# Attention of a two-layer decoder trunk: heads by quarters, with the projections cut into pieces between the heads' stages

## The chip, the cores and the metric

One core of a Trainium2 chip runs the whole program in one launch. The metric is the device time of one execution in microseconds. Before the change it was 1347.86 us, the median of 3 runs (1347.23 to 1348.67).

## The reference, cut to what matters

The input is a sequence of 512 tokens of width 1024 in float32. Layer 0 is a recurrent mixer (an RG-LRU and a Mamba-2 SSD side by side) followed by a dense SwiGLU network; layer 1 is an attention layer followed by a second SwiGLU network. The change is in the attention layer alone:

```python
h = rmsnorm(x, norm_g)
qkv = (h @ w_qkv).reshape(b, l, 3, 16, 64)
q = partial_rope(rmsnorm(qkv[:, :, 0], q_norm), pos) * (64 ** -0.5)   # rope on the first 16 of 64
k = partial_rope(rmsnorm(qkv[:, :, 1], k_norm), pos)
v = qkv[:, :, 2]
# softmax attention over three dilated windows, (128, 1), (512, 4), (2048, 16),
# merged by their softmax denominators
...
return x + o @ w_out
```

There are 16 heads of 64 channels. The three windows are merged into one softmax: the kernel adds the logarithm of how many windows hold a key (a table `lnc`, -1e30 where none does) to the scores.

## The kernel before, in words

Every large product is made in three parts to keep float32 precision: each operand is split into a rounded high part and a low part, and the matmuls xh\*wl, xl\*wh and xh\*wh are added up in PSUM. A weight tile of 128x1024 is loaded by a DMA on SP's queue (line 105), its high part is cast by ScalarE and its low part is subtracted by VectorE, or by GpSimd for the attention weights (lines 87 to 91). `weight(i)` returns tile i and at the same time issues tile i+2; three tiles of each kind are held.

In the attention layer the queries, keys and values are projected for 8 heads at a time (`qkv_part`, a half): the stationary operand is a 128-token block of the input, the moving operand 512 columns of the weight. `finish_qk` then works on one 128-token block of q or k: ScalarE scales the block and squares it, VectorE sums the squares per head, GpSimd raises them to -1/2, VectorE multiplies and makes six small rotary operations. `pair_T` transposes q and k of two heads (four transposes each) and splits them into high and low parts; both parts of q lie on the 128 rows that the array sums over, so that two matmuls make a block of scores instead of three. `scores(h)` makes the four blocks of query rows of one head (128, 256, 384 and 512 keys wide, causal), and then for each a custom VectorE reduction, a ScalarE exponential, a reciprocal, and a GpSimd multiplication by it. `values(h)` transposes the probabilities in three groups (`P_AT`), splits each, and multiplies them with v. `out_proj` makes two output tiles of 128 channels from one weight tile and four pairs of heads.

The order written is: the three projections of half 0, its 8 heads, the three projections of half 1, its 8 heads with the first half's output projection between them, and the second half's output projection. This order is not the one in which the engines run: the framework keeps a list of what is written, and puts an instruction on its engine when its inputs are ready by the framework's own estimate, earlier written ones first. Each engine then runs its list in order, and waits on semaphores. So the projections of half 1 run between the heads of half 0.

PSUM has eight banks: four for projections (`pa`), three for transposes and scores (`pm`), one for the values' sums (`po`). Lines that the steps below touch: 96 to 109 (`weight`), 709 (rotary tables), 721 to 743 (projections), 747 to 768 (`finish_qk`), 770 to 788, 790 to 796 (`finish_v`), 806 to 860, 862 to 898.

Of the kernel before, what the change touches and what calls it, by code (L numbers as in the profile page):

```python
# [58 lines left out]
def trunk(ctx: ExitStack, tc: tile.TileContext, a):  # L59
# [36 lines left out]
    def weight(i):  # L96
        while emitted[0] <= min(i + AHEAD, len(specs) - 1):
# [11 lines left out]
        return w_of.pop(i, None)  # L109
# [578 lines left out]
    with ExitStack() as actx:  # L688
# [9 lines left out]
        tabs = {}  # L698
        for w, (gn, rn, scale) in enumerate((("q_gain", "q_rope", 0.125), ("k_gain", "k_rope", 1.0))):
# [5 lines left out]
            g1 = pc(rn, 0, 8).rearrange("p (o e) -> p o e", o=1).to_broadcast([P, NT, 8])  # L705
            g2 = pc(rn, 8, 8).rearrange("p (o e) -> p o e", o=1).to_broadcast([P, NT, 8])
            for nm, trig, gg in (("c1", cos, g1), ("s2", sin, g2), ("c2", cos, g2), ("s1", sin, g1)):
                t = am.tile([P, NT, 8], F32, name=f"rope{w}{nm}", bufs=1)
                V.tensor_tensor(out=t, in0=trig, in1=gg, op=ALU.mult)
                tabs[w, nm] = t  # L710

        qkT = {}
        vt = {}


        kz = [[ap_.tile([P, T], F32R, name=f"kz{b}{e}") for e in range(2)] for b in range(2)]
# [4 lines left out]
        def qkv_part(half, w):  # L721

            pss = []

            def step(kp):
                if kp == 0:
                    for t in range(NT):
                        pss.append(pa.tile([P, T], F32, tag="pa", name="ps_qkv"))
                wh, wl = weight(i_qkv[half, w, kp])
                for t in range(NT):  # L730
                    ts_ = slice(t * P, (t + 1) * P)
                    for k2 in range(2):
                        k = 2 * kp + k2
                        xh, xl = norm.hl[k]
                        cols = slice(k2 * T, (k2 + 1) * T)
                        mm(pss[t], lhsT=xl[:, ts_], rhs=wh[:, cols], start=(k == 0), stop=False)  # L736
                        mm(pss[t], lhsT=xh[:, ts_], rhs=wl[:, cols], start=False, stop=False)  # L737
                        mm(pss[t], lhsT=xh[:, ts_], rhs=wh[:, cols], start=False, stop=(k == KD - 1))  # L738
                if kp == 3:
                    for t in range(NT):  # L740
                        (finish_v if w == 2 else finish_qk)(half, w, t, pss[t])

            return [lambda kp=kp: step(kp) for kp in range(4)]

        qk = {}

        def finish_qk(half, w, t, ps):
            q = at.tile([P, 8, 64], F32, tag=f"q{w}{t}", name="q", bufs=2)
            qf = q.rearrange("p h e -> p (h e)")
            S.activation(qf, ps, AF.Copy, scale=norm.rt[:, t:t + 1])  # L750
            sq = at.tile([P, 8, 64], F32, tag="qsq", name="qsq", bufs=1)
            S.activation(sq.rearrange("p h e -> p (h e)"), qf, AF.Square)
            ss = am.tile([P, 8], F32, tag="qss", name="qss")
            V.tensor_reduce(out=ss, in_=sq, axis=AX.X, op=ALU.add)
# [10 lines left out]
            V.tensor_tensor(out=tmp[:, 3], in0=x1, in1=tb("s1"), op=ALU.mult)  # L765
            V.tensor_tensor(out=x1, in0=tmp[:, 0], in1=tmp[:, 1], op=ALU.subtract)  # L766
            V.tensor_tensor(out=x2, in0=tmp[:, 2], in1=tmp[:, 3], op=ALU.add)
            qk[half, w, t] = q

        def pair_T(pair):  # L770
            half, p = pair // 4, pair % 4
# [221 lines left out]
```

## Time and profile before

| | |
|---|---|
| runs, median | 1347.86 us |
| profiled execution, own time | 1346.39 us |
| its span, first to last instruction | 1344.6 us |
| PE (matmul) busy | 1318.4 us, 98% |
| PEld (weight load) busy | 1072.5 us, 80% |
| DVE (VectorE) busy | 796.2 us, 59% |
| ACT (ScalarE) busy | 573.4 us, 43% |
| POOL (GpSimd) busy | 151.7 us, 11% |
| granted TensorE clock | 0.999 of full speed |

The profiled execution is 1.47 us below the median of the runs, and its span is 1.8 us shorter than its own time. Matmuls are pipelined: one is shown as 0.39 us long where the next starts 0.23 us later, so the busy share of PE says that it seldom stood still, and not that it ran at its best spacing. The spacing of the starts is what to read. The attention layer is the stretch from 717 to 978 us.

### The profile page before, as it was taken

Reading aid. Unit: us, or ns where it says so; the run is one execution under the profiler, and the core shown is the slowest. Engines: PE = TensorE matmul, PEld = TensorE weight load, DVE = VectorE, ACT = ScalarE, POOL = GpSimd, SP = SyncE. Lnnn points to the kernel's source line nnn. Section 1 sums busy time; section 2 is a strip of 40 time slices with the busy share of each in tenths; the row PEclk is TensorE's granted clock in tenths of the full one; section 3 lists DMA queues with packets and bytes.
Section 4 is the critical chain, followed back from the end, with each engine's and each line's share of the span. In section 5 each row is a group of like instructions: output and inputs, shape, how many; then the busy total and the mean of one; then the engine's idle time right before and its main releaser. Section 6 shows DMA issues by size and latency. Waiting matters only on the chain.

```text
span 1344.6 us, 15688 instructions
## 1 busy us (share of the span) xinstructions
PE 1318.4 (98%) x6058; PEld 1072.5 (80%) x6058; DVE 796.2 (59%) x1332; ACT 573.4 (43%) x842; POOL 151.7 (11%) x130
## 2 busy tenths in 40 slices
PE   8999989999999999999999999999999999999998
PEld 6877767788888888888888877777788888888887
DVE  6886799975454434434453778788764434443442
ACT  5743867443333222322243379558643212222321
POOL 0000000000000000000005755554300000000000
PEclk9999999999999999999999999999999999999999
DMA  6322222532323323233232221121032323323232
GB/s 239 111 80 93 95 79 71 174 101 94 94 94 94 95 96 102 89 106 94 89 100 94 90 68 47 63 78 48 32 108 96 94 95 96 100 87 110 94 95 78
DMA packets 38555, 126.50 MB, mean 94 GB/s; under 512 B 4289, under 2 KB 5057, under 8 KB 38353
## 3 DMA queue, kind: packets, MB, share of 16 engines
q1 hardware_dynamic: 38480, 125.51, 29.2%
q8 instruction: 47, 0.77, 0.2%
q14 instruction: 28, 0.22, 0.0%
HBM read 123.36 MB, written 2.13 MB: 93 GB/s over the span
## 4 chain that ended last, share of the span: by engine, by line
PE 81%; DVE 9%; ACT 6%; POOL 2%; issue 1%; DMA 0%; SPq 0%; POOLq 0%; DVEq 0%; ACTq 0%
PE ps_pr L113 24%; PE ps_pr L114 24%; PE ps_pr L115 24%; ACT s L825 2%; POOL qrs L757 1%; DVE q L758 1%; PE ps_qkv L738 1%; PE ps_qkv L737 1%; PE ps_qkv L736 1%; DVE q L766 1%; ACT ph L90 1%; PE ps_o L852 1%; PE ps_pT L845 1%; ACT qk_hi L783 1%; DVE rtmp L762 1%
## 5 line engine op out<-in xcount | busy, mean ns | idle before, releaser
L90 ACT CAST wh<-wr 128x1024 fp32r<-128x1024 f32 (+2 forms) x223 | 228.2, 1025 | 621.3 <-PE ps_pr L115 388.2
L113 PE MATMUL ps_pr<-xh,wl 128*128 128x512 f32 x1056 | 416.5, 395 | 12.7 <-DVE wl L91 12.0
L114 PE MATMUL ps_pr<-xl,wh 128*128 128x512 f32 x1056 | 414.5, 392 | 0.9 <-DVE xl L191 0.9
L115 PE MATMUL ps_pr<-xh,wh 128*128 128x512 f32 x1056 | 413.2, 391 | 0.0
L91 DVE TENSOR_TENSOR wl<-wr,wh 128x1024 fp32r<-128x1024 f32 (+2 forms) x191 | 225.6, 1182 | 52.3 <-ACT wh L90 51.9
L113 PEld LDWEIGHTS ps_pr<-xh,wl 128*128 128x128 f32 x1056 | 199.4, 189 | 55.5 <-DVE wl L91 12.9
L114 PEld LDWEIGHTS ps_pr<-xl,wh 128*128 128x128 f32 x1056 | 199.5, 189 | 43.5 <-DVE xl L191 1.8
L115 PEld LDWEIGHTS ps_pr<-xh,wh 128*128 128x128 f32 x1056 | 199.3, 189 | 42.4 <-issue 0.6
L113 PE MATMUL ps_pr<-ah,wl 128*128 128x512 f32 x352 | 136.9, 389 | 0.0
L114 PE MATMUL ps_pr<-al,wh 128*128 128x512 f32 x352 | 136.9, 389 | 0.0
L115 PE MATMUL ps_pr<-ah,wh 128*128 128x512 f32 x352 | 136.9, 389 | 0.0
L91 POOL TENSOR_TENSOR wl<-wr,wh 128x1024 fp32r<-128x1024 f32 x32 | 78.4, 2453 | 392.3 <-ACT wh L90 392.2
L670 DVE TENSOR_TENSOR tu<-ps_pr,nrb 128x512 f32<-128x512 f32 x44 | 30.4, 691 | 130.7 <-PE ps_pr L115 130.7
L678 DVE TENSOR_TENSOR x<-ps_pr,x 128x512 f32<-128x512 f32 x48 | 33.2, 692 | 120.4 <-PE ps_pr L115 120.3
L668 DVE TENSOR_TENSOR tg<-ps_pr,nrb 128x512 f32<-128x512 f32 x44 | 30.4, 691 | 94.1 <-PE ps_pr L115 94.1
L114 PEld LDWEIGHTS ps_pr<-al,wh 128*128 128x128 f32 x352 | 66.1, 188 | 13.8
L115 PEld LDWEIGHTS ps_pr<-ah,wh 128*128 128x128 f32 x352 | 66.1, 188 | 13.7
L113 PEld LDWEIGHTS ps_pr<-ah,wl 128*128 128x128 f32 x352 | 66.1, 188 | 13.7
L736 PE MATMUL ps_qkv<-wh,xl 128*128 128x512 f32 x192 | 75.6, 394 | 0.5 <-ACT q L750 0.5
L737 PE MATMUL ps_qkv<-wl,xh 128*128 128x512 f32 x192 | 75.5, 393 | 0.0
L738 PE MATMUL ps_qkv<-wh,xh 128*128 128x512 f32 x192 | 75.5, 393 | 0.0
L736 PEld LDWEIGHTS ps_qkv<-wh,xl 128*128 128x128 f32 x192 | 36.1, 188 | 7.9 <-ACT q L750 1.0
(233 smaller groups left out, 1575.2 us busy)
## 6 DMA issues: line engine op xcount, KB each, us to landing
wr<-in_w_gu SPq DMA_DIRECT2D x88, 512.0 KB, 3.5
wr<-in_w_in SPq DMA_DIRECT2D x35, 512.0 KB, 3.5
wr<-in_w_dn SPq DMA_DIRECT2D x32, 448.0 KB, 3.2
wr<-in_w_qkv SPq DMA_DIRECT2D x24, 512.0 KB, 3.5
wr<-in_w_out SPq DMA_DIRECT2D x16, 512.0 KB, 3.5
wr<-in_w_dn SPq DMA_DIRECT2D x16, 512.0 KB, 3.4
x<-in_xT SPq DMA_DIRECT2D x16, 256.0 KB, 3.7
bcs<-csd SPq DMA_DIRECT2D x16, 256.0 KB, 4.4
```

Of the source, the lines that this page charges most:

```text
L90: S.copy(hi, src)
L91: eng.tensor_tensor(out=lo, in0=src, in1=hi.bitcast(F32), op=ALU.subtract)
L113: mm(ps, lhsT=wl[ws], rhs=xh[xs], start=start, stop=False)
L114: mm(ps, lhsT=wh[ws], rhs=xl[xs], start=False, stop=False)
L115: mm(ps, lhsT=wh[ws], rhs=xh[xs], start=False, stop=stop)
L668: V.tensor_tensor(out=tg, in0=pg, in1=rb, op=ALU.mult)
L670: V.tensor_tensor(out=tu, in0=pu, in1=rb, op=ALU.mult)
L678: V.tensor_tensor(out=x[m], in0=ps, in1=x[m], op=ALU.add)
L736: mm(pss[t], lhsT=xl[:, ts_], rhs=wh[:, cols], start=(k == 0), stop=False)
L737: mm(pss[t], lhsT=xh[:, ts_], rhs=wl[:, cols], start=False, stop=False)
L738: mm(pss[t], lhsT=xh[:, ts_], rhs=wh[:, cols], start=False, stop=(k == KD - 1))
L825: S.activation(s, s, AF.Exp, scale=-1.0, bias=m[:, 0:1], accum_out=m[:, 1:2])
```

## The change

The attention layer is rewritten; everything ahead of it and behind it stays.

- q, k and v are projected for 4 heads at a time (a quarter). One weight tile holds 256 columns of q and 256 of k for two blocks of the inner dimension, so q and k of a quarter are still matmuls of 512 columns. v of a quarter has 256 columns, and its matmuls are 256 wide: 384 of them, where there were 192 of 512.
- The projections are lists of short pieces: a piece of q and k is 6 matmuls of 512 columns (one token block, two inner blocks), one of v is 12 of 256 columns (one token block, four inner blocks), one of the output projection is 6 of 512. `fill_in` writes the next pieces between the steps of the heads.
- Heads go by pairs. A pair's twelve steps hold the transposes and values of both its heads and, between them, `pair_T` and `scores` of the next pair. With each pair 12 pieces are written for the first five, then 4, 5 and 4.
- q and k of a quarter are finished together: one power on GpSimd for 128x32 sums in place of four for 128x8, four multiplications, and four rotary operations over all four token blocks with two prepared tables (32 small multiplications at the start, where there were 8). Of these the VectorE operations are written through a queue, two behind each piece.
- `scores` takes both heads of a pair together, in three groups, with two PSUM banks at a time; one reciprocal serves a group. The transposed probabilities have one buffer of each kind instead of two.
- A weight tile two ahead is issued behind the second piece of the tile in work, instead of ahead of its first.

The diff, cut to its core (removed functions stand in the listing above):

```diff
     def weight(i):
-        while emitted[0] <= min(i + AHEAD, len(specs) - 1):
+        weight_emit(i + AHEAD)
+        return weight_get(i)
+    def weight_get(i):
+        return w_of.pop(i, None)
+    def weight_emit(i):
...
-    i_qkv = {}
-    for half in range(2):
-        for w in range(3):
-            for kp in range(4):
-                i_qkv[half, w, kp] = add_spec(a["w_qkv"][w * 2 + half, kp], D)
+    i_qkv = {(g, c): add_spec(a["w_qkv"][g, c], D) for g in range(4) for c in range(6)}
...
+        cc = at.tile([P, NT, 8, 16], F32, name="rope_c", bufs=1)
+        sc = at.tile([P, NT, 8, 16], F32, name="rope_s", bufs=1)
...
+            for half in range(2):
...
+                for t in range(NT):
+                    for tab, trig, gx in ((cc, cos, gg), (sc, sin, ng)):
+                        V.tensor_tensor(
+                            out=tab[:, t, 4 * w:4 * w + 4, es],
+                            in0=trig[:, t].rearrange("p (o e) -> p o e", o=1).to_broadcast([P, 4, 8]),
+                            in1=gx.rearrange("p (o e) -> p o e", o=1).to_broadcast([P, 4, 8]), op=ALU.mult,
+                        )
...
+        def qk_pieces(g):
...
+            def piece(kp, t):
+                i = i_qkv[g, kp]
+                if t == 0:
+                    w_cur[i] = weight_get(i)
...
+                    mm(pss[t], lhsT=xl[:, ts_], rhs=wh[:, cols], start=(k == 0), stop=False)
...
+                if t == 1:
+                    weight_emit(i + AHEAD)
+                if kp == 3:
+                    finish_a(t)
+            def finish_a(t):
...
+                S.activation(qf, pss[t], AF.Copy, scale=norm.rt[:, t:t + 1])
...
+                S.activation(sq.rearrange("p h e -> p (h e)"), qf, AF.Square)
+                queue.append(lambda: V.tensor_reduce(out=sqs["ss"][:, t], in_=sq, axis=AX.X, op=ALU.add))
+                if t == NT - 1:
+                    queue.append(finish_b)
...
+            def finish_b():
...
+                G.tensor_tensor(out=rs.rearrange("p t h -> p (t h)"), in0=ss, in1=mhalf[:, :NT * 8], op=ALU.pow)
+            def finish_c(t):
...
+                V.tensor_tensor(out=q, in0=q, in1=sqs["rs"][:, t].rearrange("p (h o) -> p h o", o=1).to_broadcast([P, 8, 64]), op=ALU.mult)
...
+            def finish_d():
...
+                V.tensor_tensor(out=c, in0=q[:, :, 0:16], in1=cc.rearrange("p t h e -> p (t h) e"), op=ALU.mult)
+                V.tensor_tensor(out=s, in0=q[:, :, 0:16], in1=sc.rearrange("p t h e -> p (t h) e"), op=ALU.mult)
+            def finish_e():
+                q, c, s = views()
+                V.tensor_tensor(out=q[:, :, 0:8], in0=c[:, :, 0:8], in1=s[:, :, 8:16], op=ALU.add)
+                V.tensor_tensor(out=q[:, :, 8:16], in0=c[:, :, 8:16], in1=s[:, :, 0:8], op=ALU.add)
...
         def v_pieces(g):
...
+            def piece(vp, t):
...
+                ps = pss[t][:, :256]
+                for k4 in range(4):
...
+                    mm(ps, lhsT=xl[:, ts_], rhs=wh[:, cols], start=(k == 0), stop=False)
...
+                if vp == 1:
+                    v = ap_.tile([P, 4, 2, 64], F32R, tag=f"v{t}", name="v", bufs=2)
...
+            return [lambda vp=vp, t=t: piece(vp, t) for vp in range(2) for t in range(NT)]
...
+        S_AT = {0: ((3, 0),), 1: ((0, 0), (2, P)), 2: ((1, 0),)}
+        P_AT = {0: ((0, 0),), 1: ((1, 0), (3, 3 * P)), 2: ((2, 0),)}
...
+        def scores(p, b):
...
+            pss = [pm.tile([P, T], F32, tag="pm", name="ps_s") for _ in range(2)]
+            for i, c in S_AT[b]:
...
+                    mm(pss[e][:, c:c + n], lhsT=q[e][:, qs], rhs=kl[e][:, :n], start=True, stop=False)
+                    mm(pss[e][:, c:c + n], lhsT=q[e][:, qs], rhs=kh[e][:, :n], start=False, stop=True)
...
+                    if c == 0:
+                        prob[2 * p + e, "s", b] = at.tile([P, WID[b]], F32, tag=f"s{b}", name="s", bufs=4)
...
+                    V.tensor_tensor_reduce(out=s, in0=ps, in1=lnc[:, T - n:], scale=-1.0, scalar=-NEG, op0=ALU.add, op1=ALU.min, accum_out=m[:, 0, u:u + 1])
+                    S.activation(s, s, AF.Exp, scale=-1.0, bias=m[:, 0, u:u + 1], accum_out=m[:, 1, u:u + 1])
...
+            V.reciprocal(m[:, 2, :k], m[:, 1, :k])
+            for u, s in enumerate(done):
+                G.tensor_scalar(out=s, in0=s, scalar1=m[:, 2, u:u + 1], scalar2=1.0, op0=ALU.mult, op1=ALU.mult)
+        def turn(h, b):
+            ps = pm.tile([P, T], F32, tag="pm", name="ps_pT")
...
+            hi = at.tile([P, WID[b]], F32R, tag=f"ph{b}", name="ph", bufs=1)
+            lo = at.tile([P, WID[b]], F32R, tag=f"pl{b}", name="pl", bufs=1)
+            split(ps[:, :WID[b]], hi, lo)
+            p_hl[h, b] = (hi, lo)
...
+                mm(po[:, j * P:], lhsT=v, rhs=lo[:, c:c + n], start=(j == 0), stop=False)
+                mm(po[:, j * P:], lhsT=v, rhs=hi[:, c:c + n], start=False, stop=(b == 2))
+            if b < 2:
+                return
...
+        def ao_pieces(half, after=None):
...
+                for k in (2 * kk, 2 * kk + 1):
...
+                    mm3(st["ps"], w_cur[i], oT[4 * half + k], (slice(None), slice(c, c + P)), (slice(None), slice(None)), k == 0, k == 3)
+                if m2 == 0 and kk == 1:
+                    weight_emit(i + AHEAD)
+                if kk == 1:
...
+            return [lambda mp=mp, m2=m2, kk=kk: piece(mp, m2, kk) for mp in range(4) for m2 in range(2) for kk in range(2)]
+        pieces = []
+        def fill_in(n=1):
+            for _ in range(min(n, len(pieces))):
+                pieces.pop(0)()
+                drain(2)
+        pieces += qk_pieces(0)
+        fill_in(4)
+        norm.finish()
+        fill_in(12)
+        pieces += v_pieces(0)
+        fill_in(8)
+        drain(len(queue))
+        pieces += qk_pieces(1)
+        fill_in(2)
+        pair_T(0, 0)
+        pair_T(0, 1)
+        fill_in(3)
+        for b in range(3):
+            scores(0, b)
+            fill_in(2)
+        fill_in(1)
+        for p in range(8):
+            g = p // 2
+            if p % 2 == 0 and g < 3:
+                pieces += v_pieces(g + 1)
+            elif p % 2 == 1 and g < 2:
+                pieces += qk_pieces(g + 2)
+            elif p == 5:
+                pieces += ao_pieces(0)
+            n = [12, 12, 12, 12, 12, 4, 5, 4][p]
+            nxt = p < 7
+            ha, hb = 2 * p, 2 * p + 1
+            steps = [
+                [lambda: turn(ha, 0)],
+                [lambda: turn(ha, 1)] + ([lambda: pair_T(p + 1, 0)] if nxt else []),
+                [lambda: values(ha, 0), lambda: turn(ha, 2)],
+                [lambda: values(ha, 1)] + ([lambda: pair_T(p + 1, 1)] if nxt else []),
+                [lambda: values(ha, 2)],
+                [lambda: turn(hb, 0)],
+                [lambda: scores(p + 1, 0)] if nxt else [],
+                [lambda: values(hb, 0), lambda: turn(hb, 1)],
+                [lambda: scores(p + 1, 1)] if nxt else [],
+                [lambda: values(hb, 1), lambda: turn(hb, 2)],
+                [lambda: scores(p + 1, 2)] if nxt else [],
+                [lambda: values(hb, 2)],
+            ]
+            for k, fs in enumerate(steps):
+                for f in fs:
+                    f()
+                fill_in(n * (k + 1) // 12 - n * k // 12)
+        fill_in(len(pieces))
+        assert not queue
+        pieces += ao_pieces(1, norm3.feed)
+        fill_in(len(pieces))
```

The functions `ao_pieces`, `pair_T` and `values` otherwise compute what `out_proj`, `pair_T` and `values` did. The host lays the weight of q, k and v out by quarters.

## Rows read from the trace of the kernel before

**Rows 1.** Busy time by stretch of the attention layer, all engines; (x) counts instructions.

```profile
core 0: us, PE busy (x) PEld busy (x) DVE busy (x) ACT busy (x) POOL busy (x), PEclk, DMA share, GB/s
717.40:787.40 70.00, 69.46 (x314) 57.15 (x313) 42.94 (x82) 28.00 (x37) 46.31 (x25) 1.00 0.30 98
787.40:857.80 70.40, 66.29 (x358) 51.23 (x356) 58.45 (x177) 61.09 (x135) 38.74 (x42) 1.00 0.15 46
857.80:893.40 35.60, 35.60 (x164) 29.66 (x163) 23.62 (x47) 14.89 (x20) 21.41 (x10) 1.00 0.25 82
893.40:963.00 69.60, 67.66 (x367) 52.33 (x365) 55.08 (x156) 56.67 (x129) 28.81 (x37) 1.00 0.13 42
```

**Rows 2.** Projection matmuls by line: count, ns min/median/max, first and last start.

```profile
L736 PE MATMUL ps_qkv<-wh,xl x192: 387/389/504, 717.4 to 892.0; 128*128 128x512 f32 x192
...
L115 PE MATMUL ps_ao<-xh,wh x64: 387/389/475, 894.0 to 977.9; 128*128 128x512 f32 x64
```

**Rows 3.** TensorE timeline: start us, us, engine, line, operation [idle before <- releaser].

```profile
846.80 0.33 PE L852 MATMUL ps_o<-pl,v 128*128 128x256 f32 x1
846.97 0.28 PE L853 MATMUL ps_o<-ph,v 128*128 128x256 f32 x1
847.09 0.22 PE L818 MATMUL ps_s<-kz,qk_hi 128*128 128x128 f32 x1
...
847.78 0.28 PE L819 MATMUL ps_s<-qk_hi 128*128 128x256 f32 x1
847.90 0.60 PE L845 MATMUL ps_pT<-cst,s 128*128 128x128 f32 x4
848.26 0.47 PE L737 MATMUL ps_qkv<-wl,xh 128*128 128x512 f32 x1
848.57 0.39 PE L738 MATMUL ps_qkv<-wh,xh 128*128 128x512 f32 x1
...
849.26 0.39 PE L738 MATMUL ps_qkv<-wh,xh 128*128 128x512 f32 x1
851.96 0.44 PE L845 MATMUL ps_pT<-cst,s 128*128 128x128 f32 x2 [2.30 <-DVE m L824]
```

**Rows 4.** The same view in the output projection: eight starts on from the first.

```profile
975.88 0.39 PE L115 MATMUL ps_ao<-xh,wh 128*128 128x512 f32 x1
...
977.70 0.39 PE L114 MATMUL ps_ao<-xl,wh 128*128 128x512 f32 x1
```

**Rows 5.** Timeline of the same stretch, POOL and DVE.

```profile
846.70 2.39 POOL L91 TENSOR_TENSOR wl<-wr,wh 128x1024 fp32r<-128x1024 f32 x1
846.98 2.20 DVE L766 TENSOR_TENSOR q<-rtmp 128x64 f32<-128x64 f32 x1
```

**Rows 6.** DVE multiplications of finished q and k, from source views of two lines.

```profile
L758 DVE TENSOR_TENSOR q<-q,qrs x16: 673/693/2878, 740.5 to 883.4; 128x512 f32<-128x512 f32 x16
...
L766 DVE TENSOR_TENSOR q<-rtmp x16: 206/226/2430, 742.3 to 891.6; 128x64 f32<-128x64 f32 x16
```

**Rows 7.** Waits in the attention layer: total us, times, longest us.

```profile
DVE q L758 <- POOL qrs L757: 16.5, 12, 1.8
```

**Rows 8.** POOL groups of the attention layer: count | busy us, mean ns | idle before.

```profile
L91 POOL TENSOR_TENSOR wl<-wr,wh 128x1024 fp32r<-128x1024 f32 x31 | 76.0, 2455 | 48.4 <-ACT wh L90 48.3
L757 POOL TENSOR_TENSOR qrs<-qss,mhalf 128x8 f32<-128x8 f32 x16 | 26.6, 1661 | 19.9 <-DVE qss L755 18.8 <-DVE m L826 1.0
...
L217 POOL TENSOR_TENSOR nrt<-rv,mhalf 128x4 f32<-128x4 f32 x1 | 1.0, 1013 | 2.0 <-DVE rv L215 2.0
```

**Rows 9.** ACT groups of the same stretch.

```profile
L90 ACT CAST wh<-wr 128x1024 fp32r<-128x1024 f32 x33 | 34.6, 1052 | 43.6 <-PE ps_qkv L738 24.1 <-issue 11.4 <-POOL wl L91 3.3
...
L750 ACT ACTIVATE q<-ps_qkv,nrt 128x512 f32<-128x512 f32 x16 | 11.0, 684 | 0.9 <-PE ps_qkv L738 0.8
```

**Rows 10.** DVE groups of the same stretch.

```profile
L754 DVE TENSOR_REDUCE qss<-qsq 128x8 f32<-128x512 f32 x16 | 10.9, 679 | 17.8 <-ACT qsq L752 17.7
```

**Rows 11.** Rotary tables, source view of their line.

```profile
L709 DVE TENSOR_TENSOR rope0c<-cst,pv x2: 182/182/182, 17.1 to 22.9; 128x32 f32<-128x32 f32 x2
```

More of the change, by code (lines that the diff above doesn't have):

```diff
@@ L719, in trunk @@
                 G.memset(kz[b][e][64 - 64 * e:128 - 64 * e].bitcast(mybir.dt.uint32), 0)
-        def qkv_part(half, w):
-            pss = []
[L725 to L743, printed above, removed]
@@ new lines, in trunk, with pair_T @@
+        w_cur = {}
+        def pair_T(p, w):
+            g, pp = p // 2, p % 2
+            o = w * 256 + pp * P
+            ps = pm.tile([P, T], F32, tag="pm", name="ps_qT")
+            for t in range(NT):
+                nc.tensor.transpose(ps[:, t * P:(t + 1) * P], qk[g][:, t].rearrange("p h e -> p (h e)")[:, o:o + P], ident)
+            hs_ = [ap_.tile([P, T], F32R, tag=f"hi{w}{e}", bufs=2, name="qk_hi") for e in range(2)]
+            klo = None if w == 0 else kz[p % 2]
+            for e in range(2):
+                own = slice(64 * e, 64 * e + 64)
+                other = slice(64 - 64 * e, 128 - 64 * e)
+                S.activation(hs_[e][own], ps[own], AF.Copy, scale=gains[w][own])
+                lo = hs_[e][other] if w == 0 else klo[e][own]
+                V.scalar_tensor_tensor(out=lo, in0=ps[own], scalar=gains[w][own], in1=hs_[e][own].bitcast(F32), op0=ALU.mult, op1=ALU.subtract)
+                if w == 1:
+                    S.activation(hs_[e][other], ps[own], AF.Copy, scale=gains[w][own])
+            qkT[p, w] = hs_ if w == 0 else (hs_, klo)
@@ L860, in values @@
                 oT.append((hi, lo))
-        def out_proj(half, mp, after=None):
-            w = weight(i_ao[half, mp])
-            for m2 in range(2):
-                ps = pa.tile([P, T], F32, tag="pa", name="ps_ao")
-                for k in range(4):
-                    c = (m2 * 4 + k) * P
-                    mm3(ps, w, oT[4 * half + k], (slice(None), slice(c, c + P)), (slice(None), slice(None)), k == 0, k == 3)
-                m = 2 * mp + m2
-                V.tensor_tensor(out=x[m], in0=ps, in1=x[m], op=ALU.add)
-                if after is not None:
-                    after(m)
@@ L874, in trunk @@
-        for w in range(3):
-            for st in qkv_part(0, w):
-                st()
-                if norm.rt is None:
-                    norm.finish()
-        def attend(half, between):
-            first = 8 * half
-            pair_T(first // 2)
-            scores(first)
-            for h in range(first, first + 8):
-                if h % 2 == 0 and h < first + 6:
-                    pair_T(h // 2 + 1)
-                if h < first + 7:
-                    scores(h + 1)
-                values(h)
-                for st in between.get(h, ()):
-                    st()
@@ L977 @@
         "w_out": np.stack([_tiles(n["rec_w_out"][0][h * D:(h + 1) * D], 8) for h in range(2)]),
[L978 removed]
+        "w_qkv": np.stack([_quarter(n["att_w_qkv"][0].reshape(D, 3, 4, 256)[:, :, g]) for g in range(4)]),
         "w_ao": n["att_w_out"][0].reshape(2, 4, P, 4, 2, P).transpose(0, 3, 2, 4, 1, 5).reshape(2, 4, P, 8 * P),
```

221 lines of the change are left out of this document (107 added, 114 removed).

## The prediction

> **What bounds the kernel now.** I read the busy time by stretch first, then where each line of the attention layer starts and ends, then the spacing of TensorE's starts, then the waits. The layer runs from 717.4 us, the first projection, to about 978.1, where the last output matmul (977.9) has its successor [rows 2]: 260.7 us. In its two dense stretches, 70.0 and 35.6 us of projections, TensorE is never idle for long and ScalarE is at 28.0 and 14.9 us, under half. In the two stretches of heads it is the other way: ScalarE 61.1 of 70.4 and 56.7 of 69.6 us, VectorE 58.5 and 55.1 [rows 1]. So TensorE bounds the layer as a whole, but among the heads it runs at the pace of two helpers that are 80 to 87% busy, and four pairs of heads take 70 us, 17.5 a pair, in both halves.
>
> How much of the 260.7 us is waiting? What the matmuls need at their unhindered spacing: eight starts of 512 columns take 977.70 - 975.88 = 1.82 us, 0.2275 each [rows 4], times 576 + 192 (three lines of 192 and of 64 [rows 2]): 174.7. A head's score matmuls of 128, 256 and 384 columns run from 847.09 to 847.90, 0.81 us [rows 3]; with two of 512, 1.27. The values have the same widths, so 16 x 2 x 1.27 = 40.6. Four transposes take 0.36 us, 0.09 each [rows 3]; 224 of them, 20.2. The eight small matmuls of the norm are taken at 0.1: 0.8. Sum 236.3, so 24.4 us are lost. Part of that can't go: behind each group of transposes the next matmul starts its successor 0.31 instead of 0.2275 us later [rows 3], and there are 64 groups (three a head, two a pair), 5.3 us. That leaves 19.1 us of waits, and this is all that a new order can win.
>
> The longest wait shows the mechanism. TensorE stood 2.30 us before a transpose at 851.96 [rows 3]. A rotary addition of 64 columns, which takes 0.21 us at best, took 2.20 because it met GpSimd's 2.39 us weight split [rows 5, 6], and the scores' reductions stood behind it in VectorE's list.
>
> **The change part by part.** *Pieces between the steps.* The counts of score, value and transpose instructions on TensorE stay. Projections of q and k and the output projection stay at 512 columns. What moves is slack: in the old list a head's step follows as soon as its inputs are estimated ready, and any lateness on the chip is a stall. With a piece (6 x 0.2275 = 1.37 us) written ahead of the next step, that much lateness is hidden. A pair needs (40.6 + 20.2) / 8 = 7.6 us of TensorE plus 0.7 for eight switches. The first five pairs get 12 pieces each, 16.4 us or more, so 24.7 us: well over the 17.5 at which the helpers have kept up. The waits of a pair were about 2 us (19.1 over eight pairs, with the two ends in it). I put these five at 0.7 each, not 0: at the pair's boundary the last scores need reduction, exponential, reciprocal and GpSimd's multiplication before the next pair's first transposes, with only two pieces and one short step between. If the slack hides nothing it is 2 each, if it hides all, 0. Together 3.5.
>
> *Pairs 5 and 6* have only 4 and 5 pieces: 8.3 + 5.5 = 13.8 and 15.1 us of TensorE. At 17.5 us a pair they would lose 3.7 + 2.4 = 6.1 us. Output pieces written for later can be pulled ahead, so I take 5. The start of the heads: the finish of quarter 0 (below) takes 17 us, under 8 pieces of v and two of q and k, 14.2; three more pieces are ready, so I take 1, between 0 and 3. The end (the last pair's output, the first FFN matmuls) has the same dependences as before: 1.8, as part of the 19.1.
>
> So 3.5 + 5 + 1 + 1.8 = 11.3 us of waits stay, and 19.1 - 11.3 = 7.8 are won.
>
> *v in 256 columns.* 192 matmuls go, 43.7 us, and 384 of half the width come. The nearest rows, 256 columns between others, are spaced 0.12 (847.78 to 847.90) and 0.17 us (846.80 to 846.97) [rows 3]. The first is a matmul of that width whose weight load lay beside its predecessor, as in a steady run; the second follows two matmuls of 128. I take 0.12: 46.1, a cost of 2.4. Below it the bound is 0, at half of the 0.2275 of twice the columns [rows 4]. Above it 0.17: 65.3, a cost of 21.6.
>
> *Finishing per quarter.* It removes 12 of 16 power instructions and 96 rotary operations, and adds 8 and 8 of wider ones; the 16 multiplications stay. GpSimd's power took 1.013 us for 4 columns and 1.661 for 8 [rows 8], 0.16 a column; for 32 I estimate 5.5 us from these two, 22 in all against 26.6. The chain for a quarter: two ScalarE passes 1.4 [rows 9], the sum 0.7 [rows 10], a wait for a weight split on GpSimd of 1.2 on average (half of 2.455 [rows 8]), the power 5.5, four multiplications and two rotary ones at 0.67 (the smallest of the 512-wide ones [rows 6]) and two additions at half that, 4.7, and one or two meetings with a weight split at 2.2, 3.3: 17 us. For quarters 1 to 3 eight pieces and more lie behind the last q and k piece before `pair_T` needs them, about 18 us; cost 0, and rival 2 has what it costs if that cover fails. What stands behind the wait on VectorE is the scores' reductions and the splits of the probabilities, and TensorE waits for those.
>
> *Rotary tables.* 32 small VectorE instructions instead of 8, at 0.18 us [rows 11]: 4.3 us more. VectorE has 27 us free in the first dense stretch [rows 1]; 0, or 4.3 if they land in the opening of the kernel, where the old ones ran. *Reciprocals*: 24 for 64, off the path; 0, between 0 and 1 either way since a group now waits for its last exponential.
>
> *Weights two pieces later.* 24 + 8 tiles as before, same bytes and same SP queue. A tile's cast (1.05) and split (2.46) [rows 8, 9] must fit in the 2.7 + 5.5 us that stay ahead of its use in the dense start; they do. SP's own issue hangs on the buffers, not on TensorE. 0; if the 5.5 us power sits in front of a split there, up to 4, once. *One buffer for transposed probabilities* instead of two: values of a group come three steps before the next transposes of that group; 0.
>
> Sum on the profiled execution: 1346.39 - 7.8 + 2.4 = 1341.0 us. The median of the runs is 1.47 above the profile: 1342.5.
>
> **The rivals.** *1, nothing is won.* ScalarE's and VectorE's work is all still there, and the waits reappear at the pair boundaries and in pairs 5 and 6 at 17 instead of 11.3 us. For it: the 17.5 us a pair in both old halves. Against it: nearly 25 us a pair now. 19.1 - 17 = 2.1 won, 2.4 lost: 1348.
>
> *2, slower, VectorE held by the quarter's power.* VectorE already waited 16.5 us in 12 times for the 1.66 us powers [rows 7]. With 5.5 us, and if the list puts the multiplications too early, each of the quarters 1 to 3 stalls the reductions by about 4 us and the start by 4: 16 us. It decides as soon as the chain is longer than the 18 us of cover. 7.8 - 16 - 2.4 gives a loss of 10.6: 1358.5. The Trainium skill, page "SBUF — State Buffer", section "SBUF: two separate sides", says that a VectorE instruction with two SBUF inputs and a GpSimd one that reads SBUF lock each other out for a whole instruction. By that rule the trace agrees, 0.21 to 2.43 us for one form [rows 6]; and the 32 finishing instructions that stay are all of that kind, so the chain would lengthen where splits are dense.
>
> *3, slower, v pays its loads.* Each 256-wide matmul at 0.17 us: 1342.5 + 21.6 - 2.4 = 1362. It decides from 0.134 a matmul, where v costs the 7.8 us that the order wins. For it: all rows of 256 columns stand alone. Against it: at 512 columns the load of 0.19 us is hidden entirely, since the spacing is 0.2275. The Trainium skill, "TensorE: Matmul & The Clock Gate", Part 3, "The mechanism", has weight loads beside running matmuls only when the row groups differ, and these all take the full array; the 512-wide spacing disagrees with it here.
>
> *4, nearly all is won*: 5 us of waits stay: 19.1 - 5 - 2.4 = 11.7, 1336.
>
> **How the numbers follow.** Forecast (1338 to 1345) 0.45, rival 4 0.13, rival 1 0.22, rival 2 0.14, rival 3 0.06. A measurement of this kernel tells 0.2%, 2.7 us, from no change. Faster by more: 0.45 + 0.13 = 0.58; within: 0.22; slower: 0.14 + 0.06 = 0.20. The range leaves out most of rival 3, half of rival 2 and the lucky end of rival 4: 1335 to 1357.
>
> **What would show it.** Right: the layer from the first projection to the last output matmul about 255 us; v's matmuls 0.12 us apart; the heads spread over some 200 us with ScalarE near 80% throughout; no waits over 1 us in the first five pairs, most of the loss in pairs 5 and 6. Wrong: VectorE waiting more than 3 us for a power with TensorE idle beside it; v spaced 0.15 or more; waits of 2 us or more at each pair's first transposes.

## The result, and the profile after

The changed kernel takes 1378.7 us (median of 4 runs, 1378.2 to 1381.2) against 1347.6 for the kernel before in the same comparison: 1.0233 times as long, 95% interval 1.0215 to 1.0251. The forecast was 1342.5, and 1378.7 is outside its range.

First the windows, the layer by stretch and then four stretches cut at the changes of the granted clock (the columns are those of [rows 1]):

```profile
717.40:751.40 34.00, 33.74 (x198) 29.59 (x196) 13.04 (x44) 13.48 (x20) 22.09 (x11) 1.00 0.29 90
751.40:798.40 47.00, 39.02 (x208) 32.99 (x208) 24.37 (x49) 27.48 (x49) 18.08 (x14) 0.93 0.18 56
798.40:860.30 61.90, 53.28 (x312) 46.73 (x312) 37.66 (x81) 39.19 (x80) 28.44 (x24) 0.94 0.17 52
860.30:922.00 61.70, 53.10 (x312) 46.56 (x312) 37.66 (x81) 39.19 (x80) 28.42 (x24) 0.94 0.16 52
922.00:1011.00 89.00, 79.51 (x417) 65.16 (x418) 66.25 (x136) 54.98 (x115) 32.98 (x33) 0.96 0.18 54
...
755.33:762.16 6.83, 3.42 (x8) 2.75 (x9) 4.46 (x10) 0.00 (x0) 0.00 (x0) 0.50 0.22 77
803.12:809.95 6.83, 4.97 (x20) 4.87 (x21) 6.46 (x20) 3.33 (x9) 3.04 (x3) 0.50 0.20 73
864.56:871.39 6.83, 4.56 (x18) 4.45 (x19) 6.83 (x21) 3.34 (x9) 2.62 (x3) 0.50 0.21 77
926.00:932.83 6.83, 4.31 (x17) 4.20 (x18) 6.83 (x21) 3.29 (x9) 2.38 (x3) 0.50 0.23 77
```

The layer ends at 1011 instead of 978: 293.6 us for 260.7. ScalarE is down to 63% among the heads (39.2 of 61.9), where it was at 87% [rows 1], and VectorE and TensorE are at smaller shares too: somebody waits. And four times the granted clock is 0.50, the 1.2 GHz level, where the layer before had 1.00 in all four stretches of [rows 1]. In these four stretches TensorE works 17.3 us at half speed, 8.6 more than the same work takes at full speed. That is an upper bound of what the clock costs: in three of the four VectorE is busy 6.46 to 6.83 of the 6.83 us, so TensorE would not have run freely there at full speed either.

Then the waits of the layer, total, times and longest:

```profile
PEld ps_s L877 <- DVE m L889: 21.9, 6, 7.0
PE ps_s L877 <- DVE m L889: 20.5, 4, 6.8
DVE q L790 <- POOL qrs L785: 19.6, 4, 5.5
...
PE ps_qkv L759 <- DVE v L837: 7.6, 1, 7.6
```

TensorE waits 6.8 us three times for a score reduction and 7.6 once for the eviction of v; VectorE waits four times for the power. It was 16.5 us in 12 times before [rows 7], so the total grew by only 3.1 us. The timeline around the second power, VectorE, GpSimd and TensorE, tells what changed:

```profile
793.97 0.16 DVE L783 TENSOR_SCALAR qss<-qss 128x32 f32<-128x32 f32 x1
794.31 0.69 DVE L91 TENSOR_TENSOR pl<-ps_pT,ph 128x512 fp32r<-128x512 f32 x1 [0.17 <-ACT ph L90]
799.68 4.63 DVE L790 TENSOR_TENSOR q<-q,qrs 128x512 f32<-128x512 f32 x4 [4.68 <-POOL qrs L785]
804.23 0.68 DVE L889 CUSTOM_DVE_ANT_0 s<-ps_s,cst 128x512 f32<-128x512 f32 x1
...
794.21 5.44 POOL L785 TENSOR_TENSOR qrs<-qss,mhalf 128x32 f32<-128x32 f32 x1 [9.53 <-DVE qss L783]
799.62 2.34 POOL L91 TENSOR_TENSOR wl<-wr,wh 128x1024 fp32r<-128x1024 f32 x1
...
797.68 0.28 PE L827 MATMUL ps_v<-wh,xl 128*128 128x256 f32 x1
797.80 0.28 PE L828 MATMUL ps_v<-wl,xh 128*128 128x256 f32 x1
797.92 0.28 PE L829 MATMUL ps_v<-wh,xh 128*128 128x256 f32 x1
804.98 0.48 PE L877 MATMUL ps_s<-kz,qk_hi 128*128 128x128 f32 x1 [6.77 <-DVE m L889]
```

The four multiplications stand in VectorE's list behind the sums' scaling, with one split of probabilities between (L91), and ahead of the score reductions (L889). They wait for the power; on GpSimd a weight split is next behind the power, so it starts (799.62) as the multiplications do (799.68), and the four take 4.63 us, where four undisturbed ones take 2.49 (e2, below). All that time the finished scores stay in their banks, and TensorE, which wants the same banks, is still from 798.2 to 804.98.

### The profile page after: what moved, and what is told of

The parts are those of the page before. It is cut to its first block, busy times and chain, and to the rows that moved or that the text cites. A ratio compares the mean times of both kernels' runs of the same rounds, so it can differ in the third digit from the quotient of the medians.

```text
span 1376.4 us, 15896 instructions
## 1 busy us (share of the span) xinstructions
PE 1324.7 (96%) x6250; PEld 1091.3 (79%) x6250; DVE 780.3 (57%) x1236; ACT 576.9 (42%) x850; POOL 143.7 (10%) x118
## 4 chain that ended last, share of the span: by engine, by line
PE 83%; DVE 6%; ACT 4%; issue 3%; POOL 3%; DMA 0%; SPq 0%; POOLq 0%; ACTq 0%
PE ps_pr L119 23%; PE ps_pr L120 23%; PE ps_pr L121 23%; POOL qrs L785 2%; DVE q L790 2%; PE ps_qkv L759 1%; PE ps_qkv L760 1%; PE ps_qkv L761 1%; ACT wh L90 1%; POOL wl L91 1%; PE ps_s L877 1%; DVE xl L91 1%; PE ps_pT L901 1%; POOL s L895 1%; PE ps_s L878 1%
## 5 line engine op out<-in xcount | busy, mean ns | idle before, releaser
L91 DVE TENSOR_TENSOR wl<-wr,wh 128x1024 fp32r<-128x1024 f32 (+2 forms) x191 | 225.9, 1184 | 53.1 <-ACT wh L90 52.7
L91 POOL TENSOR_TENSOR wl<-wr,wh 128x1024 fp32r<-128x1024 f32 x32 | 76.6, 2394 | 417.9 <-ACT wh L90 417.9
L759 PE MATMUL ps_qkv<-wh,xl 128*128 128x512 f32 x128 | 53.4, 417 | 7.6 <-DVE v L837 7.6
L890 ACT ACTIVATE s<-s,m 128x128 f32<-128x128 f32 (+3 forms) x64 | 35.5, 556 | 36.6 <-DVE m L889 36.4
L761 PE MATMUL ps_qkv<-wh,xh 128*128 128x512 f32 x128 | 50.7, 396 | 0.0
L760 PE MATMUL ps_qkv<-wl,xh 128*128 128x512 f32 x128 | 50.6, 395 | 0.0
```

Source lines behind the costliest of these rows:

```text
L91: eng.tensor_tensor(out=lo, in0=src, in1=hi.bitcast(F32), op=ALU.subtract)
L890: S.activation(s, s, AF.Exp, scale=-1.0, bias=m[:, 0, u:u + 1], accum_out=m[:, 1, u:u + 1])
```

## The experiments

Theory A is the reading above: VectorE's wait, placed ahead of the reductions. Its rivals: B, the new order of steps and pairs; C, multiplications lengthened by weight splits; D, GpSimd's own time. All stand in the expectations. A meeting, below, is a VectorE instruction that is lengthened beside a weight split of GpSimd.

**e1, the power over 8 columns.** The power of 24 of the 32 sums is left out; the multiplications of all four blocks read block 0's.

```diff
-G.tensor_tensor(out=rs..., in0=ss, in1=mhalf[:, :NT * 8], op=ALU.pow)
+G.tensor_tensor(out=rs[:, 0], in0=ss[:, 0], in1=mhalf[:, :8], op=ALU.pow)
```

> The changed kernel with the quarter's power made over 8 columns instead of 32 (block 0's sums serve all four blocks; the power of the other 24 sums is left out). The order of every engine's list is that of the changed kernel. Theory A (VectorE's list stands at the multiplications behind the quarter's power of 5.44 us, TensorE runs out of PSUM banks, and the clock falls behind it): the wait shrinks by 3.8 us a quarter, 15 us in all, and some or all of the four stretches at half clock go: 1355 to 1364. Rival B (the cause is the new order of the steps and pairs, not the power): 1372 or more. Rival C (the multiplications lengthened by GpSimd's weight splits): 1372 or more, since the splits stay.

1360.0 us. The three stalls shrink from 6.77 to 3.04, the first from 7.6 to 1.7. As theory A has it.

**e2, nobody waits for the power.** The multiplications read the sums, so the power's effect on q and k is left out.

```diff
-V.tensor_tensor(out=q, in0=q, in1=sqs["rs"][:, t]...
+V.tensor_tensor(out=q, in0=q, in1=sqs["ss"][:, t]...
```

> The changed kernel with the four multiplications of a quarter reading the sums instead of the powers, so that no instruction of VectorE waits for the power; GpSimd still makes the power of 5.4 us (its effect on q and k is left out). Every engine's list is in the changed kernel's order. Theory A (the wait): 1345 to 1353, no stall over 3 us in TensorE and no stretch at half clock. Rival D (GpSimd being taken for 5.4 us, so that its multiplications by the reciprocals and its weight splits come late): 1370 or more, since GpSimd is taken as long. Rival B (the order): about 1378.

1349.9 us, 28.8 less, with the clock at 1.00. GpSimd and VectorE at the second quarter:

```profile
785.79 5.44 POOL L785 TENSOR_TENSOR qrs<-qss,mhalf 128x32 f32<-128x32 f32 x1 [9.54 <-DVE qss L783]
...
786.50 2.49 DVE L790 TENSOR_TENSOR q<-q,qss 128x512 f32<-128x512 f32 x4
788.90 0.69 DVE L889 CUSTOM_DVE_ANT_0 s<-ps_s,cst 128x512 f32<-128x512 f32 x1
```

The multiplications run beside the power, undisturbed, and TensorE's longest wait in the layer is 1.7 us. Without the wait the loss is gone: rival B is out, and GpSimd's 5.44 us alone don't make it here (rival D). But this edit takes two things away at once, since the multiplications now begin beside the power and not beside the split behind it; e6 and e13 tell the two apart.

TensorE's matmuls come in the same order in both kernels, so their starts can be compared one by one. Around the second stall, the changed kernel first and then e2:

```profile
793.72 0.50 PE L877 MATMUL ps_s<-kz,qk_hi 128*128 128x512 f32 x1
...
821.09 0.51 PE L916 MATMUL ps_o<-pl,v 128*128 128x512 f32 x1 [1.04 <-DVE pl L91]
```

```profile
785.30 0.50 PE L877 MATMUL ps_s<-kz,qk_hi 128*128 128x512 f32 x1
...
805.66 0.50 PE L916 MATMUL ps_o<-pl,v 128*128 128x512 f32 x1 [1.06 <-DVE pl L91]
```

The lag is 8.4 us ahead of the stall and 15.4 some 16 us behind it: 7.0 for a stall of 6.77. In between it is up to 17.3 (811.59 against 794.33), but what the half clock adds there doesn't last. Counted so over the whole layer the changed kernel falls 29.9 us behind e2, of which 27.9 are the four stalls; some 2 us are left for the clock, net of small waits that only e2 has (0.62 three times), and most of them at quarter 0.

**e3, a power per token block**, 128x8 behind each block's sums.

```diff
+queue.append(lambda: finish_b(t))
-    queue.append(finish_b)
...
+G.tensor_tensor(out=sqs["rs"][:, t], in0=ss, in1=mhalf[:, :8], op=ALU.pow)
```

> The changed kernel with four powers of 128x8 a quarter, each behind its own block's sums, as the kernel before had them; all else of the quarter's finish stays. GpSimd works a little longer (4 x 1.66 against 5.44 us a quarter), but three of the four powers are done while the quarter's last piece still runs. Theory A: the wait is at most 1.7 us a quarter and no stretch at half clock is left: 1345 to 1355. Rival D (GpSimd's own time): about 1375. Rival B: 1375 or more.

1367.5 us, neither theory's number. None of VectorE's waits for a power is longer than 1.8 us, but there are 13; and quarter 0's stall is still 7.9, because two multiplications and one rotary operation of quarter 0 met weight splits (2.88, 2.82 and 2.71 us).

**e4, the power on VectorE.**

```diff
-G.tensor_tensor(out=rs..., in0=ss, in1=mhalf[:, :NT * 8], op=ALU.pow)
+rsqrt_dve(rs..., ss, 32)   # guess by bits, then 3 x (y*y, *(-v/2), (+1.5)*y)
```

> The changed kernel with the power of a quarter made on VectorE in twelve small instructions (128x32, a first guess by the bits and three Newton steps) in place of the one on GpSimd. VectorE works some 2 us longer a quarter but waits for no other engine there. Theory A: 1342 to 1353, near the 1342.5 that was forecast for the change, and the clock at 1.00 through the layer. Rival B (the order): 1370 or more. Rival C (multiplications lengthened by weight splits): 1360 or more.

1365.2 us, a miss for theory A and inside rival C's number: three stalls of 4.47 stay, though VectorE waits for no power. VectorE and GpSimd:

```profile
791.09 0.17 DVE L744 TENSOR_SCALAR qrs<-qss 128x32 int32<-128x32 int32 x1
...
791.87 2.17 DVE L745 TENSOR_SCALAR qrs<-qrs 128x32 int32<-128x32 int32 x1
...
797.75 1.83 DVE L750 SCALAR_TENSOR_TENSOR qrs<-nrt__5977,qrs 128x32 f32<-128x32 f32 x1
...
791.60 2.40 POOL L91 TENSOR_TENSOR wl<-wr,wh 128x1024 fp32r<-128x1024 f32 x1 [10.74 <-ACT wh L90]
...
797.16 2.37 POOL L91 TENSOR_TENSOR wl<-wr,wh 128x1024 fp32r<-128x1024 f32 x1
```

Two of the small instructions of some 0.2 us fall into weight splits and take 2.17 and 1.83. By the rule that the prediction cited from the Trainium skill ("SBUF — State Buffer", "SBUF: two separate sides") the loser waits for the whole instruction. The second of these rows has two SBUF inputs, as what was cited there asks, and agrees; the first has one input and was held up all the same. e2's rows differ from the rule: the power reads SBUF too, and four multiplications of two inputs ran inside it undisturbed. So rival C holds a part of the loss, which e6 and e7 measure.

**e5, the multiplications 12 pieces later; e8, v of quarter 0 ahead of its q and k as well.** In both, the finish of quarters 1 to 3 comes behind the transposes that read q and k, so these read unfinished values.

```diff
+queue.extend([lambda: None] * (24 if g else 0))
 for u in range(NT):
     queue.append(lambda u=u: finish_c(u))
```

> The changed kernel with the four multiplications and the rotary steps of quarters 1 to 3 written 12 pieces later (some 20 us), so that in VectorE's list they stand behind the scores' reductions of that pair instead of ahead of them. Same work, same power of 5.4 us on GpSimd, same collisions; quarter 0 is left as it is. Theory A (place in the list: what stands behind the waiting instruction): the three stalls of 6.8 us go, 20.3 us, and the three half-clock stretches behind them, 4.95 + 4.6 + 4.3 us of TensorE time at half speed, 6.9 us lost: about 1352, between 1348 and 1356; the stall of quarter 0 (7.6 us) stays. Rival C (VectorE's work as such, lengthened by meetings with weight splits, is too much beside the heads): the stalls come back elsewhere, 1362 or more. Rival B (the order of steps): 1372 or more.

> The changed kernel with the multiplications 12 pieces later for quarters 1 to 3, and v of quarter 0 projected ahead of its q and k, so that quarter 0's finish lies under 12 pieces of the next q and k, and no v waits behind it on VectorE (then 11 pieces instead of 12 between the heads of pairs 1 to 4). Theory A: quarter 0's stall of 7.6 us and the half clock behind it (3.5 us of TensorE time, 1.7 lost) go too: 9 us below the kernel with the late multiplications alone, about 1343, between 1338 and 1347. Rival B: 1372 or more. If the cover at the start fails in another way, 1350 or more.

1357.1 and 1357.9 us; e5 lies 1.1 above theory A's range. In e5 the three stalls of 6.8 are gone (21.6 us won of 26.7 expected), but the finish now stands beside the next pair's transposes: 4.7 us of waits for `qk_hi` and 4.6 for GpSimd's multiplications. e8 is a miss: quarter 0's stall turns into one of 4.5 at the first transposes, some 21 us (12 pieces, 16.4, and 4.5) behind the last projection of quarter 0.

**e6 and e7, no weight splits on GpSimd** in the changed kernel and in e4. GpSimd fills the low parts of the attention weights with zeros; the low parts are left out.

```diff
-eng.tensor_tensor(out=lo, in0=src, in1=hi..., op=ALU.subtract)
+G.memset(lo..., 0) if eng is G else eng.tensor_tensor(...)
```

> The changed kernel with GpSimd filling the low parts of the attention weights with zeros instead of subtracting (it reads no SBUF; the weights' low part is left out). All lists are in the changed kernel's order; the wait for the power stays 5.4 us. Theory A: only the lengthening goes, 2.1 us at each of quarters 1 to 3, 4 us at quarter 0 and some 3 us at the small stalls, and some of the clock with it: 1362 to 1370. Rival C (collisions are the cause): 1352 or less.

> The kernel with the power on VectorE in twelve small instructions (1365.2 us, stalls of 4.47 us left) with GpSimd filling the low parts of the attention weights with zeros instead of subtracting. If what is left there comes from VectorE's instructions meeting weight splits (2.17 and 1.83 us for two of the twelve where 0.2 would do), the stalls shrink to about 1 us and the clock stays: 1346 to 1353. If the burst of VectorE work ahead of the scores is enough by itself, the stalls stay over 2.5 us: 1357 or more.

1361.4 and 1348.7 us: 17.3 and 16.5 less; e6 lies 0.6 under theory A's range. The longest multiplication, from the source views of the changed kernel and of e6 (ns min/median/max):

```profile
L790 DVE TENSOR_TENSOR q<-q,qrs x16: 676/679/2868, 749.4 to 927.2; 128x512 f32<-128x512 f32 x16
```

```profile
L790 DVE TENSOR_TENSOR q<-q,qrs x16: 683/685/693, 749.1 to 911.3; 128x512 f32<-128x512 f32 x16
```

The stalls fall only to 4.65 in e6, since the wait is still there, and to 2.0 in e7, where about 1 was expected. The edit also shortens GpSimd's own work, from 2.39 us a weight to 0.95:

```profile
L91 POOL MEMSET wl<- 128x1024 uint32 x30 | 28.6, 954 | 101.8 <-PE ps_qkv L760 64.7 <-PE ps_ao L119 31.3 <-PE ps_pr L119 3.8
```

So the time that it wins is called the cost of the splits below; how much of it is meetings, and how much is GpSimd coming earlier to its other work, no run here tells.

**e9 and e10, a power per block and the last multiplications 4 pieces later**, e10 with v of quarter 0 first (and 11 pieces with pairs 1 to 4, as in e8).

> The changed kernel with a power of 128x8 for each token block, right behind that block's sums, and the last of the multiplications of quarters 1 to 3 written 4 pieces later, so that by VectorE's list the scores' reductions of 512 stand ahead of it. The result is the reference's. Against the kernel with a power per block alone (1367.5 us: stalls of 1.4 to 1.7 us, nine of them, and 7.9 at quarter 0): theory A, place in the list, has the three stalls of 1.5 us ahead of the scores and some of the others go and the clock's two short half-clock stretches with them, 5 to 10 us: 1357 to 1363; quarter 0 stays as it is. If the multiplications' work alone holds the scores: 1366 or more.

> As the kernel with a power per block and the last multiplications 4 pieces later, and v of quarter 0 projected ahead of its q and k (10 pieces of the next q and k lie under quarter 0's finish). The result is the reference's. Theory A: quarter 0's stall of 7.9 us and its half clock go: 1344 to 1350, so about as long as the kernel before. If VectorE's chain at quarter 0 is still longer than the 13.7 us of cover: 1352 or more.

1360.9 us for e9, inside theory A's numbers: the stalls of 1.5 us ahead of the scores and the half-clock stretches there are gone. e10 is a miss at 1362.6: the first transposes wait 5.4 us, and new waits of 2 to 2.9 come where its order is another. v first doesn't shorten the chain of quarter 0; it moves its cost to the first transposes.

**e11 and e12, the kernel before** with its powers on VectorE, and with four of its 16 powers made 5.5 us long.

```diff
+G.tensor_tensor(out=r4, in0=four(ss), in1=four(mhalf[:, :8]), op=ALU.pow)   # t == 3, 128x32
```

> The kernel before with its 16 powers of 128x8 made on VectorE in twelve small instructions each, so that VectorE waits for no power (it waited 16.5 us in 12 times). Theory A (what a wait costs is what stands behind it, and before only dense projections stood there, with four banks to go on): the time hardly moves, 1345 to 1350. If VectorE's waits for the power cost their length wherever they are: 1332 to 1338.

> The kernel before with the power of each fourth token block made over 32 columns (its 8 sums read four times), so that four of its 16 powers take 5.44 us instead of 1.66. Theory A: two of the four lie in the first dense stretch, where TensorE has other projections to go on with, and two near heads; 0 to 4 us more, 1348 to 1352. If a power of 5.4 us stalls TensorE wherever VectorE waits for it: 4 x 3.8 = 15 us and the clock behind, 1363 or more.

e11: 1349.2 us, 1.0008 times before (0.9999 to 1.0018). That alone doesn't show that the 16.5 us of waits of [rows 7] were free, since VectorE's 192 small instructions take 48.7 us in the layer in their place. What shows it is where the waits lie; the first and last of each dense stretch:

```profile
740.48 0.69 DVE L758 TENSOR_TENSOR q<-q,qrs 128x512 f32<-128x512 f32 x1 [1.75 <-POOL qrs L757]
...
775.62 2.88 DVE L758 TENSOR_TENSOR q<-q,qrs 128x512 f32<-128x512 f32 x1 [1.25 <-POOL qrs L757]
...
871.12 0.69 DVE L758 TENSOR_TENSOR q<-q,qrs 128x512 f32<-128x512 f32 x1 [1.82 <-POOL qrs L757]
...
883.42 2.88 DVE L758 TENSOR_TENSOR q<-q,qrs 128x512 f32<-128x512 f32 x1 [1.25 <-POOL qrs L757]
```

All 12 lie there, and TensorE was busy 69.46 of 70.00 and 35.60 of 35.60 us in these stretches [rows 1]: it lost 0.5 us at most.

e12: 1363.1, 14.9 more, and theory A was wrong there. GpSimd and TensorE in the dense stretch, and then TensorE's waits in the layer:

```profile
751.17 5.52 POOL L762 TENSOR_TENSOR qr<-qss,mhalf 128x32 f32<-128x32 f32 x1 [0.89 <-DVE qss L755]
756.66 7.47 POOL L91 TENSOR_TENSOR wl<-wr,wh 128x1024 fp32r<-128x1024 f32 x3
...
759.06 0.50 PE L737 MATMUL ps_qkv<-wl,xh 128*128 128x512 f32 x1 [1.93 <-POOL wl L91]
```

```profile
PE ps_qkv L737 <- POOL wl L91: 6.0, 3, 2.2
...
PE ps_pT L851 <- POOL s L833: 3.4, 2, 2.7
```

Here the power makes GpSimd late, not VectorE: three splits stand behind it, and TensorE waits for the first (and the clock is at 0.50 behind three of the stalls). Rival D is right for the kernel before. There a long instruction cost more by what stands behind it on its own engine than by what waits for it.

**e13 and e14, what the order is worth.** The open point was why e2 came to 1349.9 and not to 1342.5. e13 is e2, and e14 the kernel before, both with e6's edit.

> The changed kernel in which neither the multiplications wait for the power (they read the sums; GpSimd still makes the power) nor GpSimd subtracts for the low parts of the attention weights (it fills them with zeros). Compared with the kernel before that has the same zeros (below): if the order wins the 7.8 us of the prediction less the 2.4 us of v's narrower matmuls, it comes out 5 us below that one, 1334 to 1340. If the order wins nothing and the meetings with the splits are what is left in both, it comes out within 2 us of it, 1341 to 1346.

> The kernel before with GpSimd filling the low parts of the attention weights with zeros instead of subtracting (the low parts are left out). The 2.3 us stall that a 2.2 us rotary addition made goes, and what else the meetings cost: 1340 to 1346, 2 to 8 us below the kernel before. If the meetings cost TensorE nothing but that one stall: 1346 to 1348.

1339.8 and 1342.7 us. The splits cost 10.1 us in the changed kernel without the wait (1349.9 - 1339.8) and 5.8 before (1348.4 - 1342.7). Without wait and splits the change wins 2.9; with v's 2.4 on top, the order wins 5.3.

e13 also parts the two things that e2 took away at once. Without splits the wait costs 21.6 us (e6 - e13, 1361.4 - 1339.8), with them 28.8: the wait by itself is the larger part, and 7.2 come with the splits, which it makes the multiplications meet.

**e15 to e18, toward a better kernel.** e15: e4 with the multiplications 4 pieces later. e16: e15 with the attention's weight splits on VectorE. e17: as e16, 5 pieces. e18: the kernel before with powers and splits on VectorE.

```diff
-    on_pool = ("in_w_qkv", "in_w_ao")
+    on_pool = ()
```

> The changed kernel with the power on VectorE in twelve small instructions (1365.2 us, three stalls of 4.47 us ahead of a score matmul) and the multiplications of quarters 1 to 3 written four pieces later, so that two of them stand behind the next group's scores. The result is the reference's. Theory A (place in the list): the three stalls and most of the half clock behind them go, 13.4 and 3 to 5 us: 1346 to 1351. If the work and the meetings decide: the stalls move to the place where the multiplications now stand, 1357 or more.

> As the kernel with the power on VectorE and the multiplications four pieces later, with the attention weights' low parts subtracted by VectorE too (1.22 us each against 2.39 on GpSimd; 32 of them, 39 us of 261, VectorE then some 80% busy). The result is the reference's. GpSimd reads two SBUF inputs nowhere in the layer, so no instruction of VectorE is lengthened: no VectorE multiplication above 0.8 us. If the meetings are what is left: 1338 to 1346, below the kernel before. If VectorE's own time becomes the bound among the heads: 1352 or more.

> As e16 (power and weight splits on VectorE), with the multiplications of quarters 1 to 3 five pieces later instead of four, which puts the last two of the four behind the reductions of 256 instead of ahead of them. The result is the reference's. Theory A: the three stalls of 1.73 us go or fall under 0.5: 4 to 5 us below e16, 1340 to 1343. If they come from elsewhere: 1345 to 1347.

> The kernel before with its powers (twelve small instructions each) and the attention weights' low parts made by VectorE, as in e16. The result is the reference's. If the new order is worth some 3 to 5 us, as e13 against e14 has it: 1346 to 1352, above e16. If e16's gain is only the two moves: 1341 to 1345, e16's time or below.

e15: 1364.7 us, theory A wrong. The clock stays at 1.00, but where three stalls of 4.47 were there are now waits of 0.5 to 1.8 us between 797 and 931 us: seventeen, 17.5 us in all, against eight with 16.4 in e4. With meetings in the stretch, another place in the list only moved the loss here; in e9 it had won 6.7. e16: 1345.9, 0.9983 times before (0.9975 to 0.9992). e17: 1343.7, 0.9967 (0.9954 to 0.9979), the shortest time of a kernel that does the whole computation. VectorE's splits in e17 (count, ns min/median/max), and the longest of its TensorE's waits:

```profile
L91 DVE TENSOR_TENSOR wl<-wr,wh x34: 1212/1224/1459, 723.2 to 983.7; 128x1024 fp32r<-128x1024 f32 x34
```

```profile
PE ps_pT L913 <- POOL s L907: 4.7, 5, 1.3
```

e16's three stalls of 1.73 are 1.3 in e17, where under 0.5 was expected, and 1343.7 lies just above theory A's range. The longest multiplication of e16 is 1.03 us, not under 0.8 as expected. e18: 1347.2, 0.9994 (0.9985 to 1.0003): the two moves alone win nothing that can be told from none, so the 3.5 us by which e17 is shorter belong to the rest of the change, the order above all.

## Why the prediction was wrong

**The step that failed** is "for quarters 1 to 3 eight pieces and more lie behind the last q and k piece before `pair_T` needs them, about 18 us; cost 0". The cover held. In quarter 1 the last q and k matmul, the finish's last instruction and the first transpose of q stand so:

```profile
789.20 0.40 PE L761 MATMUL ps_qkv<-wh,xh 128*128 128x512 f32 x1
...
807.80 0.41 DVE L807 TENSOR_TENSOR q<-rc,rs 128x256 f32<-128x256 f32 x1
...
818.06 0.27 PE L849 MATMUL ps_qT<-cst,q 128*128 128x128 f32 x1
```

The chain took 18.6 us (17 were estimated), the transpose came 28.5 us behind that matmul, 6.8 of them the stall, and waited for nothing. But the cost was not 0. The step asked when the result of the chain is needed. What decided is where the waiting instruction stands: VectorE runs its list in order, and the score reductions stood behind it, while TensorE had 4.2 us left (794.0 to 798.2) before it needed their banks. The prediction named them in its next sentence and gave them no price. The stalls were 6.77 three times and 7.61, 27.9 us, and some 2 more lasted from the half clock (under e2); e2 takes away 28.8.

**Rival 2 had the mechanism** at 0.14, with too low a price: 16 against 28.8, or 21.6 where no split is met. Its condition was wrong too: it was to decide "as soon as the chain is longer than the 18 us of cover", while in e1 the chain of quarter 1 is 14.9 us and in e6 16.5, and stalls of 3.04 and 4.65 are left. The length of the wait decides, beyond what TensorE has in hand before it needs a score bank: e1's power, 3.8 us shorter, took 3.7 off each stall of 6.77, and e6's multiplications, 2.1 shorter, took 2.1 off. Its price had left out that the split queued behind the power meets the multiplications, and the clock.

**The order won 5.3 and not 7.8** (e13, e14, both without splits), and the changed kernel pays 4.3 more for splits (10.1 - 5.8), which the sum didn't hold. So the account is 28.8 (wait and clock) + 4.3 (splits) + 2.4 (v) - 5.3 (order) = 30.2 of the 31.1 measured. It adds up because its terms are differences of the same five kernels; it sorts the loss and doesn't test it. The 19.1 us that the prediction held for waits were got by subtraction: the trace of the kernel before lists only 7.1 us of TensorE waiting in the layer. What the other 12 are stays open.

Without the wait the time would have been near rival 1's (1348; e2 has 1349.9), but by luck: rival 1 had the order win nothing, while here it won and the splits took that back.

**What held:** the power of 32 columns took 5.44 us (estimate 5.5). v's matmuls start 0.12 us apart (797.68, 797.80, 797.92 above), so rival 3 is out. No matmul of the changed kernel waits long for a weight; the later weights cost nothing. TensorE's waits at the transposes of the probabilities stayed below 0.5 us. "VectorE waiting more than 3 us for a power with TensorE idle beside it" was named as the sign of the error, and it is the row at 799.68.

## What to carry to other kernels

Price a wait by what stands behind the waiting instruction in its engine's list, not by when its own result is needed: 16.5 us of waits in front of dense projections cost TensorE 0.5 us at most, and 19.6 us in front of the score reductions cost 28.8. Joining four short operations into one long one saves busy time (21.7 for 26.6 us) and makes one long wait of four short ones. Where two engines' instructions can hold each other up, a wait for the helper also sets the moment of the meeting: what the helper does next begins as the waiter does (799.62 and 799.68 above).

## What the runs showed of the hardware

A stall can bring the clock down: in each of the four stalls of 6.8 to 7.6 us the granted clock fell to 0.50, and stayed there for 6.83 us, beyond the stall's end. It also fell beside two of e7's three stalls of 2.0 us, both of e12's of 1.9 and, each behind a row of three, two of e3's stalls of 1.5. It did not behind e15's, the longest 1.76, e12's 2.18 or the 2.30 of [rows 3]. So the length of one stall doesn't tell whether the clock falls. What the half clock costs isn't TensorE's loss at that rate either: of 8.6 us some 2 lasted. The Trainium skill, "TensorE: Matmul & The Clock Gate", Part 1, "What's actually happening", says that the half rate is the default and activity releases it; the four stretches, each begun while TensorE stood still, agree.
